# Strassen stages with reused weights, and one block's split weights kept in DRAM

## The chip, the core and the metric

One program runs on one core of a Trainium2 chip. Its engines each run their own instructions in order: TensorE (PE, matrix products), VectorE (DVE), ScalarE (ACT), GpSimd (POOL); SyncE (SP) issues all transfers of this kernel, also in order. DRAM is the memory outside the core, to and from which 16 DMA engines carry data. The metric is the time of one execution on the device in microseconds, lower is better.

## The reference

Three transformer blocks in a row on 1024 tokens of width 1024, all in float32. Cut to its products:

```python
x = x + mix(rms(x) @ w_in) @ w_out                  # block 1: two kinds of attention
x = x + square(relu(rms(x) @ w_up)) @ w_down        # w_up 1024 x 4096
x = rms(x)
q, k, v, ga, gb, pool, su, sv, gates = split(rms(x) @ w_in_2)   # block 2
y = concat(neighborhood(q, k, v), conv(ga * sigmoid(gb)), pooled(pool), gating(su, sv))
x = rms(x + (y * silu(gates)) @ w_out_2)
x = x + rms(mix3(rms(x) @ w_in_3) @ w_out_3)        # block 3
x = x + rms(cross_attention(rms(x), memory))
u = causal_conv3(rms(x) @ w_up_3)                   # 1024 x 5632, gate and value halves
x = x + rms((gelu(gate) * value) @ w_down_3)
```

## The kernel before

Activations lie transposed, 128 features by 1024 tokens a tile, and are worked on in two halves of 512 tokens (h = 0, 1). A float32 product is made of parts: each operand is split into hi (rounded to the matmul's type) and lo (the rest), and `mm3` (L177) issues hi·hi, hi·lo and lo·hi (L179, L180, L181), each of 512 columns. `dense` runs it over 8 feature tiles: 24 matmuls for an output tile of one half.

**Weights.** `chunk` (L147) loads 512 KB of a weight into `raw` (two buffers), ACT copies it to `whi` (L143), DVE or, with `pool_lo`, POOL subtracts to get `wlo` (L145); whi and wlo have two buffers each. Inside `with e.third()` there is a third pair in a pool "wx", opened and closed there. So whi of a chunk can't be written until PE is done with the chunk two before (three before, in third).

**Order.** The program is built under a scheduler that sets each engine's order from a simulated timeline; on the chip every engine then keeps that order and waits on semaphores. A transfer that waits holds all transfers behind it on SP. Transfers report on eight lanes (DMAHW0 to 7 in the listings).

**The stages around the change**, with their place in the trace (us):
- Block 1, up product with Strassen (to 921): first n0 = 6 chunks for each half in the ordinary way (12 units), in which the norm's late steps (`steps`) and, in the second half, the sums of activations that Strassen needs (`right_forms`) and of weights (`left_forms`) are spread one step a unit; then 13 Strassen units of 7 products instead of 8.
- Block 1, down product (921 to 1271): six groups (6, 6, 5, 5, 5, 5 input tiles) of eight output tiles by two halves. `FfnDown.run` loads one chunk of weights for two products, and beside them loads and splits the next group's activations (`nq`, `up`).
- Block 2 (1271 to 1802): gated units, values, q and k for both halves (`glu`, `values`, `qk`), with the convolution of the gated unit as DVE and POOL work beside them; then pooling, gating, the convolution's output, attention with the gates (`silu`), and the output product. It loads 32 different weight chunks, 18 of them twice: 50 loads, 32 of which serve a single product of 24 matmuls. POOL makes the wlo of 24.
- Block 3, up product (2666 to 3123): n0 = 4 pairs of a gate and a value tile in the ordinary way, 16 units of 24 matmuls, then 18 Strassen units of 84; the causal convolution, gelu and the product of gate and value run on ACT and DVE behind each unit (L1897 to L1917), and the result is stored to `upd` in DRAM.
- Block 3, down product (3134 to 3380), inside `e.third()`; the pool "str" of the Strassen stage has just been closed, and "wx" takes memory that it held.

Of the kernel before, what the change touches and what calls it, by code (L numbers as in the profile page):

```python
# [18 lines left out]
P = 128  # L19
# [39 lines left out]
class Env:  # L59
# [87 lines left out]
    def chunk(self, src, shape=(8, P), pool_lo=False):  # L147

        nc = self.nc
        shape = [P] + list(shape)  # L150
        raw = self.wp.tile(shape, F32, tag="raw", name="raw")
        nc.sync.dma_start(raw, src)
        self.turn = (self.turn + 1) % (2 + len(self.wx))
        wp = self.wp if self.turn < 2 else self.wx[0]
        hi, lo = (wp.tile(shape, F32R, tag=t, name=t) for t in ("whi", "wlo"))
        self.split(hi, lo, raw, pool_lo=pool_lo)
        return hi, lo

    def kept(self, src, a, b):
# [191 lines left out]
def block1(e, next_gain):  # L351
# [328 lines left out]
    with ExitStack() as c2:  # L680
# [11 lines left out]
        forms, left = iter(()), iter(())  # L692
        units = [(f, h) for h in range(2) for f in range(n0)]
        wc = e.chunk(io["w1_up"][0])
        for i, (f, h) in enumerate(units):
            if i == n0:
                for _ in steps:
                    pass
                xs = [[a[:, j] for a in acc] for j in range(2)]
                acc.clear()  # L700
                forms, left = right_forms(e, xs, hs, fm), left_forms(e, weight, 0, w, tmp)
            p = e.dense(wc, hs[h])
            if i + 1 < len(units):
                wc = e.chunk(io["w1_up"][units[i + 1][0]])
            act(f, h, p, tmp.tile([P, HALF], F32, tag="c", name="c"))
            next(steps, None)
            next(forms, None)
            if h and f >= n0 - 2:
                next(left, None)
# [31 lines left out]

    return acc, out, down.run(add, end)

# [137 lines left out]


class FfnDown:

# [14 lines left out]

    def run(self, add, end):  # L900

        e, steps, f0 = self.e, iter(()), 0
        for g, n in enumerate(self.groups):
# [4 lines left out]
            for f, h in order:  # L908
                if last or h == 0:
                    w = e.chunk(self.src[f][:, f0 : f0 + n], (n, P))  # L910
                add(f, h, e.dense(w, us[h]), g)
                next(todo, None)
                next(steps, None)
                if last and f == NK - 1:
                    for _ in steps:
                        pass
                    steps = end(h)
# [55 lines left out]

def block2(e, acc, hs, steps, next_gain):
    nc, tc, io = e.nc, e.tc, e.io
# [20 lines left out]
    with ExitStack() as c2:  # L996
# [3 lines left out]
        def glu(h):  # L1000
            for b in range(2):
                pa = e.dense(e.chunk(io["w2_fm"][4 + b]), hs[h])
                pb = e.dense(e.chunk(io["w2_fm"][6 + b], pool_lo=True), hs[h])
                s = e.tsq()
# [4 lines left out]
        def values(h):  # L1009
            ws = [e.chunk(io["w2_tm"][0, q], (4, 256), pool_lo=True) for q in range(2)]  # L1010
            for t in range(4 * h, 4 * h + 4):
# [8 lines left out]
        def qk(g, i, h):  # L1020
            y = qring.next()
            p = e.dense(e.chunk(io["w2_fm"][2 * i + g]), hs[h])
            if i == 0:
# [85 lines left out]
        for b in range(2):  # L1109
            w = e.chunk(io["w2_fm"][8 + b])  # L1110
            x = e.slot("px", (T,))
# [52 lines left out]
        v2 = []  # L1164
        ws = [e.chunk(io["w2_tm"][1, q], (4, 256)) for q in range(2)]
        for t in range(8):
# [41 lines left out]
        for b in range(2):  # L1208
            w = e.chunk(io["w2_fm"][10 + b])
            for h in range(2):  # L1210
# [16 lines left out]
        def silu(f):  # L1227

            w = e.chunk(io["w2_fm"][12 + f])
            for h in range(2):  # L1230
# [26 lines left out]
        def out(f, h):  # L1257
            if h == 0:
                acc.append(e.slot("acc"))
            nc.sync.dma_start(acc[f][:, h], xd[f, :, h])  # L1260
            p = e.dense(e.chunk(io["w2_out"][f], pool_lo=True), [m[h] for m in mix], order)
            nc.vector.tensor_tensor(acc[f][:, h], p, acc[f][:, h], op=ALU.add)
# [244 lines left out]
def block3(e, acc, hs, rest, out):  # L1507
# [412 lines left out]
    with ExitStack() as c2:  # L1920
        tmp = c2.enter_context(tc.tile_pool(name="str", bufs=8))
        new = lambda: tmp.tile([P, HALF], F32, tag="c", name="c")
        n0 = 4
        fm, w = {}, {}
        weight = lambda u, i: io["w3_up"][n0 + u + 22 * i]
        forms, left = iter(()), iter(())
        units = [(b, h) for h in range(2) for f in range(n0) for b in (f, 22 + f)]
        wc = e.chunk(io["w3_up"][0])
        for i, (b, h) in enumerate(units):
            if i == 2 * n0:  # L1930
                for _ in steps:
                    pass
                forms, left = right_forms(e, xn, hs, fm), left_forms(e, weight, 0, w, tmp)
            p = e.dense(wc, hs[h])
            if i + 1 < len(units):
                wc = e.chunk(io["w3_up"][units[i + 1][0]])
            c = new()
# [3 lines left out]
            else:  # L1941
# [3 lines left out]
                put_up(b - 22, h, cg, c)  # L1945
            for _ in range(3):
                next(steps, None)
            next(forms, None)
            if h and i >= len(units) - 2:
                next(left, None)  # L1950
# [40 lines left out]

    with e.third():
        for _ in down.run(add, end):
            pass

# [49 lines left out]
def build(tc, io, out):  # L2045
    with ExitStack() as ctx:
        e = Env(ctx, tc, io)
        acc, hs, rest = block1(e, "norm_g_2")
        acc, hs, rest = block2(e, acc, hs, rest, "mix_pre_norm_3")
        block3(e, acc, hs, rest, out)  # L2050
# [18 lines left out]
```

## Time and profile before

| | us |
|---|---|
| median of three runs | 3396.5 (3394.65 to 3396.74) |
| the profiled execution | 3399.09 |
| its span in the trace | 3397.3 |
| PE busy | 3174.9 (93%) |
| DVE, ACT, POOL busy | 2119.8, 1504.1, 698.0 |

Busy PE is not PE at its best: the granted clock of TensorE has two levels, 2.4 and 1.2 GHz (1.00 and 0.50 of a stretch), and a matmul at the lower takes twice as long and counts as busy all the same. So for a stretch both the count of matmuls (x) and the clock are read. The page's mean granted clock is 0.97.

### The profile page before, as it was taken

Reading aid. Unit: us, or ns where it says so; the run is one execution under the profiler, and the core shown is the slowest. Engines: PE = TensorE matmul, PEld = TensorE weight load, DVE = VectorE, ACT = ScalarE, POOL = GpSimd, SP = SyncE. Lnnn points to the kernel's source line nnn. Section 1 sums busy time; section 2 is a strip of 40 time slices with the busy share of each in tenths; the row PEclk is TensorE's granted clock in tenths of the full one; section 3 lists DMA queues with packets and bytes.
Section 4 is the critical chain, followed back from the end, with each engine's and each line's share of the span. In section 5 each row is a group of like instructions: output and inputs, shape, how many; then the busy total and the mean of one; then the engine's idle time right before and its main releaser. Section 6 shows DMA issues by size and latency. Waiting matters only on the chain.

```text
span 3397.3 us, 43416 instructions
## 1 busy us (share of the span) xinstructions
PE 3174.9 (93%) x16044; PEld 2645.4 (78%) x16044; DVE 2119.8 (62%) x3795; ACT 1504.1 (44%) x2710; POOL 698.0 (21%) x451
## 2 busy tenths in 40 slices
PE   7999999999999998889999899989999989998997
PEld 6789877788888877667677777778887768886886
DVE  7666566654435366965776567666636687886336
ACT  4454453454532123433644565654434444454312
POOL 3000024000000004521444444435333200000001
PEclk9999999999999999899999899999999999998999
DMA  4112134433444234355644122225422432223333
GB/s 130 41 57 61 54 112 155 143 109 109 143 130 131 75 96 136 97 141 178 199 158 127 59 66 66 84 79 180 131 69 99 149 99 83 85 79 100 121 114 102
DMA packets 157572, 369.17 MB, mean 109 GB/s; under 512 B 20912, under 2 KB 29488, under 8 KB 157360
## 3 DMA queue, kind: packets, MB, share of 16 engines
q1 hardware_dynamic: 157360, 366.40, 33.8%
q8 instruction: 126, 2.06, 0.3%
q14 instruction: 86, 0.70, 0.1%
HBM read 286.64 MB, written 72.88 MB: 106 GB/s over the span
## 4 chain that ended last, share of the span: by engine, by line
PE 35%; DVE 9%; ACT 3%; issue 2%; DMA 1%; POOL 1%; SPq 0%; DVEq 0%; ACTq 0%; POOLq 0%
PE ps_d L179 10%; PE ps_d L180 10%; PE ps_d L181 10%; ACT whi L143 1%; DVE act L145 1%; DVE acc L1454 1%; POOL wlo L145 1%; PE ps_s L1737 1%; DVE hE L1723 0%; DVE wlo L145 0%; DVE hSA L1738 0%; DVE acc L1455 0%; DVE pr L1650 0%; DVE ssum L254 0%; PE ps_o L1320 0%
## 5 line engine op out<-in xcount | busy, mean ns | idle before, releaser
L143 ACT ACTIVATE whi<-raw 128x1024 fp32r<-128x1024 f32 (+2 forms) x328 | 317.3, 968 | 711.6 <-PE ps_d L180 601.9
L179 PE MATMUL ps_d<-act,whi 128*128 128x512 f32 x1280 | 512.8, 401 | 24.5 <-DVE acc L316 8.1
L181 PE MATMUL ps_d<-act,wlo 128*128 128x512 f32 x1280 | 508.4, 398 | 20.4 <-DVE wlo L145 19.5
L180 PE MATMUL ps_d<-act,whi 128*128 128x512 f32 x1280 | 508.9, 398 | 6.8 <-DVE act L145 6.7
L145 POOL TENSOR_TENSOR wlo<-raw,whi 128x1024 fp32r<-128x1024 f32 (+1 forms) x134 | 326.0, 2436 | 446.4 <-ACT whi L143 427.9
L179 PE MATMUL ps_d<-up,whi 128*128 128x512 f32 x864 | 337.5, 391 | 11.0 <-ACT whi L143 11.0
L179 PE MATMUL ps_d<-act,ws 128*128 128x512 f32 x868 | 335.0, 390 | 3.8 <-DVE sq L867 1.9
L180 PE MATMUL ps_d<-act,ws 128*128 128x512 f32 x868 | 338.4, 390 | 0.0
L180 PE MATMUL ps_d<-up,whi 128*128 128x512 f32 x864 | 337.2, 390 | 0.0
L181 PE MATMUL ps_d<-up,wlo 128*128 128x512 f32 x864 | 336.8, 390 | 0.0
L181 PE MATMUL ps_d<-act,ws 128*128 128x512 f32 x868 | 336.2, 390 | 0.0
L219 POOL TENSOR_TENSOR rr<-rv,mhalf 128x4 f32<-128x4 f32 (+1 forms) x43 | 45.6, 1060 | 1363.4 <-DVE rv L209 1177.2
L179 PEld LDWEIGHTS ps_d<-act,whi 128*128 128x128 f32 x1280 | 245.8, 192 | 80.8 <-ACT whi L143 14.6
L145 DVE TENSOR_TENSOR wlo<-raw,whi 128x1024 fp32r<-128x1024 f32 (+2 forms) x194 | 212.6, 1096 | 148.8 <-ACT whi L143 148.7
L181 PEld LDWEIGHTS ps_d<-act,wlo 128*128 128x128 f32 x1280 | 245.3, 192 | 73.9 <-DVE wlo L145 22.6
L180 PEld LDWEIGHTS ps_d<-act,whi 128*128 128x128 f32 x1280 | 245.7, 192 | 57.6 <-DVE act L145 7.5
L179 PE MATMUL ps_d<-mix,whi 128*128 128x512 f32 x512 | 201.0, 399 | 6.8 <-DVE acc L635 4.3
L181 PE MATMUL ps_d<-mix,wlo 128*128 128x512 f32 x512 | 201.6, 395 | 5.7 <-POOL wlo L145 5.7
L180 PE MATMUL ps_d<-mix,whi 128*128 128x512 f32 x512 | 203.1, 397 | 1.3 <-DVE mix L145 1.1
L179 PEld LDWEIGHTS ps_d<-up,whi 128*128 128x128 f32 x864 | 163.0, 189 | 45.6 <-ACT whi L143 11.7
L179 PEld LDWEIGHTS ps_d<-act,ws 128*128 128x128 f32 x868 | 163.2, 188 | 38.7 <-ACT ps_d L840 2.7
L181 PEld LDWEIGHTS ps_d<-act,ws 128*128 128x128 f32 x868 | 163.3, 188 | 34.1
(438 smaller groups left out, 6643.3 us busy)
## 6 DMA issues: line engine op xcount, KB each, us to landing
raw<-in_w_up SPq DMA_DIRECT2D x90, 512.0 KB, 3.9
raw<-in_w_fm SPq DMA_DIRECT2D x84, 512.0 KB, 3.8
upd<-c SPq DMA_DIRECT2D x108, 256.0 KB, 2.8
nq<-upd SPq DMA_DIRECT2D x108, 256.0 KB, 2.9
raw<-in_w_out SPq DMA_DIRECT2D x42, 512.0 KB, 3.8
xd<-acc SPq DMA_DIRECT2D x80, 256.0 KB, 2.4
raw<-in_w_down SPq DMA_DIRECT2D x64, 320.0 KB, 3.0
acc<-xd SPq DMA_DIRECT2D x64, 256.0 KB, 5.7
```

The lines of the kernel that those rows point to most:

```text
L143: nc.scalar.activation(hi, src, AF.Copy)
L145: e.tensor_tensor(lo, src, hi.bitcast(F32), op=ALU.subtract)
L179: nc.tensor.matmul(out, lhsT=wh, rhs=xh, start=start, stop=False, skip_group_check=more)
L180: nc.tensor.matmul(out, lhsT=wh, rhs=xl, start=False, stop=False, skip_group_check=more)
L181: nc.tensor.matmul(out, lhsT=wl, rhs=xh, start=False, stop=stop, skip_group_check=more)
L219: self.nc.gpsimd.tensor_tensor(r, v, self.mhalf.broadcast_to([P, n]), op=ALU.pow)
L1454: nc.vector.scalar_tensor_tensor(m, m, g[:, k : k + 1], r, op0=ALU.mult, op1=ALU.mult)
L1737: nc.tensor.matmul(s[:, blk(j, 64)], lhsT=x[:, blk(j)], rhs=xv[:, nb * j : nb * j + nb, 1], start=True, stop=True)
```

## The change

Four parts. (1) Block 1's Strassen stage: the second half's six ordinary units run in the order 4, 5, 0, 1, 2, 3, and a helper `Ahead` keeps the last two chunks, so that units 4 and 5 take the weights that the first half has just used: 10 chunk splits instead of 12. (2) Block 3's: six ordinary pairs instead of four (24 units and 16 Strassen units: 1920 matmuls instead of 1896), the second half starts with the first half's last pair, and two norm steps a unit instead of three. (3) Block 3's down product is no longer in `third`. (4) `SplitStore`: during block 1's down product block 2's 32 chunks are loaded, split by ACT and DVE, and stored as hi and lo, 1 MB each, in DRAM; block 2 then gets a chunk by two loads of 512 KB straight into whi and wlo (`ready`), 50 times, without ACT, DVE or POOL. Of block 2's edits some that repeat the same replacement of `e.chunk(...)` by `store.get(...)` are left out.

```diff
@@ -155,6 +155,17 @@
         return hi, lo
+    def ready(self, src, shape=(8, P)):
+        self.turn = (self.turn + 1) % (2 + len(self.wx))
+        wp = self.wp if self.turn < 2 else self.wx[0]
+        out = []
+        for i, t in enumerate(("whi", "wlo")):
+            w = wp.tile([P] + list(shape), F32R, tag=t, name=t)
+            self.nc.sync.dma_start(w.bitcast(F32), src[:, i].rearrange("p (a b) -> p a b", a=shape[0]))
+            out.append(w)
+        return out
...
@@ -690,8 +701,8 @@
         forms, left = iter(()), iter(())
-        units = [(f, h) for h in range(2) for f in range(n0)]
-        wc = e.chunk(io["w1_up"][0])
+        units = [(f, 0) for f in range(n0)] + [(f - 2 if f > 1 else n0 - 2 + f, 1) for f in range(n0)]
+        ahead = Ahead(e, io["w1_up"], [f for f, h in units])
         for i, (f, h) in enumerate(units):
...
@@ -699,13 +710,12 @@
                 forms, left = right_forms(e, xs, hs, fm), left_forms(e, weight, 0, w, tmp)
-            p = e.dense(wc, hs[h])
-            if i + 1 < len(units):
-                wc = e.chunk(io["w1_up"][units[i + 1][0]])
+            p = e.dense(ahead.get(i), hs[h])
+            ahead.get(i + 1)
             act(f, h, p, tmp.tile([P, HALF], F32, tag="c", name="c"))
             next(steps, None)
             next(forms, None)
-            if h and f >= n0 - 2:
+            if i >= len(units) - 2:
                 next(left, None)
...
@@ -739,7 +749,13 @@
-    return acc, out, down.run(add, end)
+    store = SplitStore(e)
+    with tc.tile_pool(name="pre", bufs=2) as pool:
+        extra = store.steps(pool)
+        rest = down.run(add, end, extra)
+        for _ in extra:
+            pass
+    return acc, out, rest, store
...
@@ -880,6 +896,54 @@
+class Ahead:
+    def __init__(self, e, src, order):
+        self.e, self.src, self.order, self.have = e, src, order, []
+    def get(self, i):
+        if i >= len(self.order):
+            return None
+        f = self.order[i]
+        for g, w in self.have:
+            if g == f:
+                return w
+        w = self.e.chunk(self.src[f])
+        self.have = self.have[-1:] + [(f, w)]
+        return w
+class SplitStore:
+    def __init__(self, e):
+        self.e, io = e, e.io
+        fm = lambda *fs: [("fm", f) for f in fs]
+        tm = lambda i: [("tm", i, q) for q in range(2)]
+        self.keys = fm(4, 6, 5, 7) + tm(0) + fm(0, 2, 1, 3, 8, 9) + tm(1) + fm(*range(10, 20)) + [("out", f) for f in range(NK)]
+        self.src = {"fm": io["w2_fm"], "tm": io["w2_tm"], "out": io["w2_out"]}
+        self.d = e.dram.tile([len(self.keys), P, 2, 1024], F32, name="wsplit")
+    def steps(self, pool):
+        e, nc = self.e, self.e.nc
+        for i, (name, *at) in enumerate(self.keys):
+            src = self.src[name]
+            for j in at:
+                src = src[j]
+            t = pool.tile([P, 2, 1024], F32R, tag="w", name="w")
+            raw = t[:, 1].bitcast(F32)
+            nc.sync.dma_start(raw, src.rearrange("p a b -> p (a b)"))
+            yield
+            e.split(t[:, 0], t[:, 1], raw)
+            nc.sync.dma_start(self.d[i], t.bitcast(F32))
+            yield
+    def get(self, *key, shape=(8, P)):
+        return self.e.ready(self.d[self.keys.index(key)], shape)
 class FfnDown:
...
@@ -897,7 +961,7 @@
-    def run(self, add, end):
+    def run(self, add, end, extra=iter(())):
...
@@ -911,6 +975,8 @@
                 next(steps, None)
+                if g:
+                    next(extra, None)
                 if last and f == NK - 1:
...
@@ -999,15 +1065,15 @@
             for b in range(2):
-                pa = e.dense(e.chunk(io["w2_fm"][4 + b]), hs[h])
-                pb = e.dense(e.chunk(io["w2_fm"][6 + b], pool_lo=True), hs[h])
+                pa = e.dense(store.get("fm", 4 + b), hs[h])
+                pb = e.dense(store.get("fm", 6 + b), hs[h])
                 s = e.tsq()
                 nc.scalar.activation(s, pb, AF.Sigmoid)
                 nc.vector.tensor_tensor(hp[b][:, h], pa, s, op=ALU.mult)
                 next(steps, None)
         def values(h):
-            ws = [e.chunk(io["w2_tm"][0, q], (4, 256), pool_lo=True) for q in range(2)]
+            ws = [store.get("tm", 0, q, shape=(4, 256)) for q in range(2)]
             for t in range(4 * h, 4 * h + 4):
...
@@ -1258,7 +1324,7 @@
             nc.sync.dma_start(acc[f][:, h], xd[f, :, h])
-            p = e.dense(e.chunk(io["w2_out"][f], pool_lo=True), [m[h] for m in mix], order)
+            p = e.dense(store.get("out", f), [m[h] for m in mix], order)
             nc.vector.tensor_tensor(acc[f][:, h], p, acc[f][:, h], op=ALU.add)
...
@@ -1920,20 +1986,19 @@
         new = lambda: tmp.tile([P, HALF], F32, tag="c", name="c")
-        n0 = 4
+        n0 = 6
         fm, w = {}, {}
         weight = lambda u, i: io["w3_up"][n0 + u + 22 * i]
         forms, left = iter(()), iter(())
-        units = [(b, h) for h in range(2) for f in range(n0) for b in (f, 22 + f)]
-        wc = e.chunk(io["w3_up"][0])
+        units = [(b, h) for h in range(2) for f in range(n0) for b in ((f - h) % n0, 22 + (f - h) % n0)]
+        ahead = Ahead(e, io["w3_up"], [b for b, h in units])
         for i, (b, h) in enumerate(units):
             if i == 2 * n0:
                 for _ in steps:
                     pass
                 forms, left = right_forms(e, xn, hs, fm), left_forms(e, weight, 0, w, tmp)
-            p = e.dense(wc, hs[h])
-            if i + 1 < len(units):
-                wc = e.chunk(io["w3_up"][units[i + 1][0]])
+            p = e.dense(ahead.get(i), hs[h])
+            ahead.get(i + 1)
             c = new()
...
@@ -1943,10 +2008,10 @@
                 put_up(b - 22, h, cg, c)
-            for _ in range(3):
+            for _ in range(2):
                 next(steps, None)
             next(forms, None)
-            if h and i >= len(units) - 2:
+            if i >= len(units) - 2:
                 next(left, None)
...
@@ -1989,9 +2054,8 @@
-    with e.third():
-        for _ in down.run(add, end):
-            pass
+    for _ in down.run(add, end):
+        pass
```

The scheduler makes of this on SP, in block 2 around `values` (raw, whi and wlo are weight tiles; wsplit is the new tensor in DRAM; vd2, qkd2 and xd2 are stores of values, q and k, and x), before:

```order
L152 DMA raw_10993<-in_w2_fm 128x1024 [waits DMAHW4_49,DVE_49]
L988 DMA xd2_10512<-acc_8368 128x512 [waits DMAHW5_49,DVE_49]
L988 DMA xd2_10512<-acc_8415 128x512 [waits DMAHW6_49,DVE_49]
L152 DMA raw_11024<-in_w2_fm 128x1024 [waits DMAHW7_49,DVE_49]
L1038 DMA qkd2_10526<-qk_10533 128x512 [waits DMAHW0_49,Activation_49]
L152 DMA raw_11058<-in_w2_fm 128x1024 [waits DMAHW4_49,DMAHW1_49,DVE_49]
L1038 DMA qkd2_10526<-qk_10533 128x512 [waits DMAHW2_49,DVE_49]
L1038 DMA qkd2_10526<-qk_10534 128x512 [waits DMAHW3_49,Activation_49]
L1038 DMA qkd2_10526<-qk_10534 128x512 [waits DVE_49]
L152 DMA raw_11089<-in_w2_fm 128x1024 [waits DMAHW7_49,DMAHW5_49,Pool_49]
```

and now:

```order
L166 DMA whi_11054<-wsplit_7989 128x1024 [waits DMAHW6_49,PE_49]
L166 DMA wlo_11056<-wsplit_7989 128x1024 [waits DMAHW7_49]
L166 DMA whi_11089<-wsplit_7989 128x1024 [waits DMAHW0_49,PE_49]
L1082 DMA vd2_10680<-nt_11050 64x256 [waits DMAHW1_49,Activation_49]
L1082 DMA vd2_10680<-nt_11050 64x256 [waits DMAHW2_49]
L166 DMA wlo_11091<-wsplit_7989 128x1024 [waits DMAHW3_49]
L1054 DMA xd2_10665<-acc_8360 128x512 [waits DMAHW4_49,DVE_49]
L1054 DMA xd2_10665<-acc_8407 128x512 [waits DMAHW5_49,DVE_49]
L166 DMA whi_11130<-wsplit_7989 128x1024 [waits DMAHW6_49,PE_49]
L166 DMA wlo_11132<-wsplit_7989 128x1024 [waits DMAHW7_49,PE_49]
```

A weight is two transfers, and the first waits for PE to leave the chunk two before, where a raw load waited for DVE or POOL to have read the raw tile two before.

On PE, at the end of block 3's last Strassen product (ps_d by ws) and the first products of its down stage (up by whi), before:

```order
L179 MATMUL ps_d_25757<-act_23166,ws_25750 128x512
L180 MATMUL ps_d_25757<-act_23166,ws_25750 128x512
L181 MATMUL ps_d_25757<-act_23166,ws_25750 128x512
L179 MATMUL ps_d_25998<-up_25836,whi_25994 128x512 [waits DMAHW4_49,DMAHW3_49,DMAHW5_49,DMAHW2_49,DMAHW6_49,DMAHW1_49,DMAHW7_49,DMAHW0_49,Activation_49]
L180 MATMUL ps_d_25998<-up_25836,whi_25994 128x512
L179 MATMUL ps_d_26024<-up_25841,whi_25994 128x512
L180 MATMUL ps_d_26024<-up_25841,whi_25994 128x512
L179 MATMUL ps_d_26055<-up_25836,whi_26051 128x512
L180 MATMUL ps_d_26055<-up_25836,whi_26051 128x512
L181 MATMUL ps_d_26055<-up_25836,wlo_26052 128x512
```

and now:

```order
L190 MATMUL ps_d_25797<-act_22858,ws_25792 128x512
L191 MATMUL ps_d_25797<-act_22858,ws_25792 128x512
L192 MATMUL ps_d_25797<-act_22858,ws_25792 128x512
L190 MATMUL ps_d_26034<-up_25875,whi_26030 128x512
L191 MATMUL ps_d_26034<-up_25875,whi_26030 128x512
L192 MATMUL ps_d_26034<-up_25875,wlo_26031 128x512
L190 MATMUL ps_d_26034<-up_25899,whi_26030 128x512
L191 MATMUL ps_d_26034<-up_25899,whi_26030 128x512 [waits DVE_49]
L192 MATMUL ps_d_26034<-up_25899,wlo_26031 128x512
L190 MATMUL ps_d_26034<-up_25928,whi_26030 128x512
L191 MATMUL ps_d_26034<-up_25928,whi_26030 128x512 [waits DVE_49]
L192 MATMUL ps_d_26034<-up_25928,wlo_26031 128x512
```

The wait on all eight lanes and ACT ahead of the first down matmul is gone, and whole products of the down stage follow one another.

On DVE, in the first groups of block 1's down product (wlo: that stage's weights; up: its activations; acc: its sums), before:

```order
L732 TENSOR_TENSOR acc_8415<-ps_d_8835,acc_8415 128x512 [waits PE_49]
L145 TENSOR_TENSOR wlo_8914<-raw_8911,whi_8913 128x640 [waits DMAHW4_49,Activation_49]
L145 TENSOR_TENSOR up_9320<-nq_9318,up_9320 128x512 [waits DMAHW0_49,Activation_49]
L145 TENSOR_TENSOR up_9348<-nq_9346,up_9348 128x512 [waits DMAHW1_49,Activation_49]
L732 TENSOR_TENSOR acc_8026<-ps_d_8861,acc_8026 128x512 [waits PE_49]
L736 TENSOR_TENSOR acc_8026<-acc_8026,sq_8878 128x512 [waits DVE_49]
L145 TENSOR_TENSOR up_9370<-nq_9368,up_9370 128x512 [waits DMAHW3_49,Activation_49]
L145 TENSOR_TENSOR up_9398<-nq_9396,up_9398 128x512 [waits DMAHW4_49,Activation_49]
L732 TENSOR_TENSOR acc_8026<-ps_d_8886,acc_8026 128x512 [waits PE_49]
L145 TENSOR_TENSOR wlo_8970<-raw_8967,whi_8969 128x640 [waits DMAHW5_49,Activation_49]
L736 TENSOR_TENSOR acc_8026<-acc_8026,sq_8903 128x512 [waits DVE_49]
```

and now, with w, a chunk of block 2 that is split in place:

```order
L145 TENSOR_TENSOR wlo_8951<-raw_8948,whi_8950 128x640 [waits DMAHW7_49,Activation_49]
L145 TENSOR_TENSOR up_9370<-nq_9368,up_9370 128x512 [waits DMAHW7_49,Activation_49]
L742 TENSOR_TENSOR acc_8018<-ps_d_8893,acc_8018 128x512 [waits PE_49]
L746 TENSOR_TENSOR acc_8018<-acc_8018,sq_8910 128x512 [waits DVE_49]
L145 TENSOR_TENSOR up_9394<-nq_9392,up_9394 128x512 [waits DMAHW1_49,Activation_49]
L742 TENSOR_TENSOR acc_8018<-ps_d_8920,acc_8018 128x512 [waits PE_49]
L145 TENSOR_TENSOR wlo_9012<-raw_9009,whi_9011 128x640 [waits DMAHW4_49,Activation_49]
L746 TENSOR_TENSOR acc_8018<-acc_8018,sq_8937 128x512 [waits DVE_49]
L145 TENSOR_TENSOR w_9483<-w_9483 128x1024 [waits DMAHW6_49,DMAHW2_49,Activation_49]
L145 TENSOR_TENSOR up_9425<-nq_9423,up_9425 128x512 [waits DMAHW4_49,Activation_49]
L742 TENSOR_TENSOR acc_8075<-ps_d_8954,acc_8075 128x512 [waits PE_49]
L145 TENSOR_TENSOR w_9538<-w_9538 128x1024 [waits DMAHW5_49,DMAHW0_49,Activation_49]
```

Between the old instructions stand the new subtractions, each behind its own load.

## Rows read from the trace of the kernel before

**Rows 1.** The page, engines and groups: busy, mean ns, idle before and its releaser.

```profile
PE 3174.9 (93%) x16044; PEld 2645.4 (78%) x16044; DVE 2119.8 (62%) x3795; ACT 1504.1 (44%) x2710; POOL 698.0 (21%) x451
L143 ACT ACTIVATE whi<-raw 128x1024 fp32r<-128x1024 f32 (+2 forms) x328 | 317.3, 968 | 711.6 <-PE ps_d L180 601.9
L145 DVE TENSOR_TENSOR wlo<-raw,whi 128x1024 fp32r<-128x1024 f32 (+2 forms) x194 | 212.6, 1096 | 148.8 <-ACT whi L143 148.7
```

**Rows 2.** Stretches: us, busy and count of PE, PEld, DVE, ACT, POOL, clock, DMA share, GB/s.

```profile
700.00:800.00 100.00, 100.00 (x443) 82.78 (x442) 44.89 (x67) 50.62 (x94) 0.00 (x0) 1.00 0.34 105
620.00:650.00 30.00, 25.89 (x102) 20.20 (x101) 24.92 (x34) 13.87 (x23) 2.86 (x2) 0.89 0.34 113
2710.00:2790.00 80.00, 65.92 (x277) 52.77 (x276) 70.64 (x122) 39.07 (x63) 1.02 (x1) 0.94 0.30 99
2674.00:2724.00 50.00, 40.52 (x183) 32.62 (x182) 43.67 (x68) 25.72 (x37) 7.61 (x6) 0.96 0.44 146
```

**Rows 3.** PE's waits, 2640 to 2800: engine, line, waited for; us, times, longest.

```profile
PE ps_d L180 <- DVE act L145: 6.7, 1, 6.7
PE ps_d L181 <- DVE wlo L145: 3.9, 1, 3.9
```

**Rows 4.** The stretch around the start of block 3's down product.

```profile
3110.00:3140.00 30.00, 17.02 (x56) 12.91 (x55) 18.19 (x36) 9.67 (x15) 0.00 (x0) 0.72 0.36 118
```

**Rows 5.** The chain of waits there: start, us, what.

```profile
3120.08 0.43 PE ps_d L180
...
3123.48 0.79 ACT c L1897
...
3131.52 2.00 DMA upd<-c
...
3133.59 0.85 ACT whi L143
...
3134.48 0.79 PE ps_d L179
```

**Rows 6.** Stretches: block 1's down, its third group, and three of dense transfers.

```profile
960.00:1210.00 250.00, 250.00 (x1104) 207.02 (x1103) 107.54 (x156) 55.81 (x84) 0.00 (x0) 1.00 0.34 106
1050.00:1104.00 54.00, 54.00 (x240) 44.72 (x239) 33.82 (x51) 12.28 (x19) 0.00 (x0) 1.00 0.53 165
2230.00:2235.00 5.00, 3.92 (x17) 3.77 (x18) 4.33 (x17) 2.52 (x8) 1.85 (x3) 0.50 1.02 415
2330.00:2340.00 10.00, 10.00 (x46) 8.29 (x45) 8.89 (x6) 3.49 (x6) 8.97 (x5) 1.00 1.03 346
10.00:20.00 10.00, 10.00 (x72) 10.00 (x72) 10.00 (x18) 5.42 (x9) 2.97 (x2) 1.00 0.92 282
```

**Rows 7.** Transfers: issues, KB each, median us to landing.

```profile
raw<-in_w_fm SPq DMA_DIRECT2D x84, 512.0 KB, 3.8
nq<-upd SPq DMA_DIRECT2D x108, 256.0 KB, 2.9
xd<-acc SPq DMA_DIRECT2D x80, 256.0 KB, 2.4
acc<-xd SPq DMA_DIRECT2D x64, 256.0 KB, 5.7
```

**Rows 8.** PE's waits, 1268 to 1500 (block 2's first products).

```profile
PE ps_d L181 <- DVE wlo L145: 12.5, 4, 6.1
PE ps_d L179 <- DVE acc L316: 8.1, 1, 8.1
PE ps_s L179 <- ACT pls L143: 7.0, 2, 3.5
PE ps_d L179 <- DVE hp L1006: 6.7, 1, 6.7
PE ps_d L179 <- ACT whi L143: 2.3, 3, 1.0
```

**Rows 9.** DVE in time there: start, us, line, operation.

```profile
1374.25 3.33 DVE L145 TENSOR_TENSOR wlo<-raw,whi 128x1024 fp32r<-128x1024 f32 x1
```

More of the change, by code (lines that the diff above doesn't have):

```diff
@@ L971, in layer_norm, with block2 @@
     nc.vector.tensor_scalar(dst, src, mv[:, 0:1], r, op0=ALU.subtract, op1=ALU.mult)
-def block2(e, acc, hs, steps, next_gain):
+def block2(e, acc, hs, steps, store, next_gain):
     nc, tc, io = e.nc, e.tc, e.io
@@ L1021, in qk @@
             y = qring.next()
-            p = e.dense(e.chunk(io["w2_fm"][2 * i + g]), hs[h])
+            p = e.dense(store.get("fm", 2 * i + g), hs[h])
             if i == 0:
@@ L1109, in block2 @@
         for b in range(2):
-            w = e.chunk(io["w2_fm"][8 + b])
+            w = store.get("fm", 8 + b)
             x = e.slot("px", (T,))
@@ L1164, in block2 @@
         v2 = []
-        ws = [e.chunk(io["w2_tm"][1, q], (4, 256)) for q in range(2)]
+        ws = [store.get("tm", 1, q, shape=(4, 256)) for q in range(2)]
         for t in range(8):
@@ L1208, in block2 @@
         for b in range(2):
-            w = e.chunk(io["w2_fm"][10 + b])
+            w = store.get("fm", 10 + b)
             for h in range(2):
@@ L1227, in silu @@
         def silu(f):
-            w = e.chunk(io["w2_fm"][12 + f])
+            w = store.get("fm", 12 + f)
             for h in range(2):
@@ L2047, in build @@
         e = Env(ctx, tc, io)
-        acc, hs, rest = block1(e, "norm_g_2")
-        acc, hs, rest = block2(e, acc, hs, rest, "mix_pre_norm_3")
+        acc, hs, rest, store = block1(e, "norm_g_2")
+        acc, hs, rest = block2(e, acc, hs, rest, store, "mix_pre_norm_3")
         block3(e, acc, hs, rest, out)
```

## The prediction

> **What bounds the kernel now.** First the page's line of busy time: PE is busy for 3174.9 of 3397.3 us [rows 1], no other engine for more than 62%. So time is won where PE stands still or runs slow, and ACT, DVE or POOL work taken away is worth only what PE waits for it. Next the stretches: in an undisturbed one PE issues 443 matmuls in 100 us at clock 1.00 [rows 2], 0.2257 us each; I call the loss of a stretch its length less 0.2257 us times its count, which takes in waits and the half clock behind them (there a matmul takes 0.43 us [rows 5]). Then PE's waits and the chain at the four places which the change touches.
>
> **Part 1, block 1's Strassen stage.** The stretch at the border of the halves holds 102 matmuls where 132.9 fit: a loss of 30.9 × 0.2257 = 7.0 us [rows 2]. Two units there now take weights that are there, so two copies and two subtractions (0.97 and 1.1 us [rows 1]) leave the engines just when they also make the right forms. The forms themselves stay. I keep 2 us of loss: −5. Bounds: −7, and 0 if the forms alone are what is late.
>
> **Part 2, block 3's.** From 2710 to 2790 PE issues 277 matmuls where 354.4 fit: a loss of 17.5 us [rows 2]. The longest wait there is for the normalised activations, 6.7 us, [rows 3], and DVE is busy 43.67 of 50 us ahead of the border [rows 2]: in eight units (8 × 24 × 0.2257 = 43.3 us of PE) it can't do the norm of the second half and the convolution's work. With twelve units PE takes 65 us, while the norm's part of DVE's work stays as it was; four more units, estimated at 3 us each (a subtraction of 1.1 [rows 1] and as much again twice for the convolution), make it about 56 us. So the norm is in time; reuse takes the new splits away. I keep 2 us: −15.5. Against that stand two Strassen units fewer and eight ordinary ones more, 24 matmuls: +5.4. Sum −10. Bounds −12 (no loss left) and +5 (the loss only moves).
>
> **Part 3, block 3's down product outside `third`.** From 3110 to 3140 PE issues 56 matmuls where 133 fit: a loss of 17.4 us [rows 4]. The chain shows why: PE's last product ends at 3123.5, ACT and DVE make the last output tile, it is stored until 3133.5, and only then ACT copies the first down chunk's whi, on which PE starts at 3134.5 [rows 5]. That whi lies in the pool that was opened on the Strassen stage's memory, and its first write waits for everything that used it; in PE's order the wait on all eight lanes stands at that matmul. Afterwards whi comes from the standing pair, and that wait is gone. Block 1 passes the same border without `third` inside a stretch at full pace. What is late next are activations from `upd`; their last tile is wanted only in a later group. I keep 1 us: −16.4. Two buffers instead of three may cost a little in the down product, but each chunk serves two products there, and group by group block 1 does so at full pace [rows 6]. Bounds −17.4 and 0.
>
> **Part 4a, the store, beside block 1's down product.** 32 chunks are read (512 KB) and written (1 MB): 32 × 1.573 = 50.3 MB. Counted in SP's order, these loads begin behind the stage's 5th weight load and end ahead of its 36th; twelve of these spans hold 36 matmuls and twenty 30, 1032 × 0.2257 = 233 us. The stage itself moves 106 GB/s [rows 6], 24.7 MB in that time. Together 75.0 MB, 322 GB/s. The trace has dense stretches of 282, 346 and 415 GB/s at a DMA share of 0.92 to 1.03 [rows 6]: at 282 the transfers take 266 us, 33 more than PE; at 346 and 415 they fit. The third group is the worst: 8 chunks and 165 GB/s × 54 us make 21.5 MB, 398 GB/s; 62 us at 346, 8 more than PE's 54, and 52 at 415. ACT and DVE have room: a chunk adds some 1 us to each in 7 to 8 us, of which DVE works 3 to 5 [rows 6]. A cycle of a staging buffer (load 3.8 us [rows 7], copy and subtraction 2, store about 5, as two 512 KB pieces in a row) is 11 us, and two buffers turn every 14 to 16. I take +6, nearest to the row of 346. Bounds 0 and +33.
>
> The stretch of 415 GB/s bears on a rule. The Trainium skill, page "DMA: Bandwidth & Descriptors", section "Specifications", gives about 358 GB/s as a core's limit to DRAM; by it the third group would take 60 us, 6 more than PE, and the rest would fit. The trace shows more than that limit for 5 us.
>
> **Part 4b, block 2's reads.** Gone: PE's waits for wlo and whi in the first products, 12.5 + 2.3 us [rows 8], made long where a subtraction stands behind the convolution on DVE or takes 3.33 us [rows 9]; behind each of the four for wlo I count ten matmuls at 0.43 instead of 0.23 us, 8 us. Also less work on DVE and POOL ahead of three other waits: 8.1 for the second half's norm, 7.0 for the pooling, 6.7 for the gated unit [rows 8]; I count 3 of each. Sum −32.
>
> Added: a load now starts when PE leaves the chunk two before, and hi lands 3.8 us later [rows 7], lo behind it: 512 KB at 282 to 346 GB/s are 1.5 to 1.9 us, so about 5.5 us. Before, the raw tile was there early and two splits of 1 us each [rows 1] followed. A single product takes 24 × 0.2257 = 5.4 us, and lo is wanted one matmul pair later: 32 such products, just covered, at 0.2 us each +6. Behind `values` and its like, where both chunks are held to the end, 1.5 us before PE runs dry: three places × 3.6 us, and half clock behind them, 2 each: +17. First loads behind other transfers on SP, at three places, +3: in all 26. Net −6. Bounds: −25 (two thirds of the added hidden by waits that come anyway) and +12 (the other waits stay as they are, and first loads cost twice as much).
>
> **Sum.** −5 − 10 − 16.4 + 6 − 6 = −31.4, on the profiled execution 3399.1 − 31.4 = 3367.7; that execution stands 2.6 us above the median of 3396.5, so 3365.
>
> **Rivals.**
> - *A: the transfers fill up in block 1's down product.* 282 GB/s instead of 346: +33 for +6, so 3392. For it: SP issues in order and a store waits for its split, so the queue isn't always full; mean share was 0.34 and would be around 1 [rows 6]. Against: the large pieces of the store should go like the fast rows.
> - *B: block 2 gains nothing.* Loads begin too late, +12 for −6: 3383. For it: the load's latency now stands in each chain; the waits for norm and pooling have other causes, too.
> - *C, the slower side: whi and wlo land late in SP's queue.* They are issued one behind another and behind waiting stores; acc<-xd, half as large, has a median of 5.7 us where it queues [rows 7]. Each us that wlo lands later than 5.5 costs 32. It decides for slower than before from (31.4 + 6.8) / 32 = 1.2 us on, wlo at 6.7; at 7.6, 3365 + 67 = 3432. Against: 3.8 us is a median over 84 loads in a queue like this.
> - *D: the border of block 3 stays.* The first whi waits for something else as long, for instance its activations: 16 back, 3381. Against: PE's order has full products there, and `up` of the first group is loaded beside the last Strassen unit.
> - *E: transfers run like the fastest row.* 415 GB/s: nothing lost in 4a, 3359. A page of the Trainium skill, "Perfetto Trace Analysis", in its note on use of DRAM above 100%, says that a core alone isn't held to its share and can reach some 120% of it; the row of 415 agrees.
>
> **How the numbers follow.** Forecast 0.48 (its own range 3351 to 3378, from the bounds of the border terms and half of 4b's), E 0.15, B 0.15, A 0.08, C 0.08, D 0.06. About 0.2% (6.8 us, 3389.7) is what a measurement of this kernel can tell. Faster: the forecast, E, D, most of B (0.13) and some of A (0.03), 0.85. Same: the rest of A and B, 0.07. Slower: C, 0.08. The low end is the forecast with 4a at nothing and 4b at −22: 3343. The high end takes in A with 2 us to spare, 3394; C lies outside.
>
> **What would show it.** Of the border terms: 2650 to 2850 without a PE wait of over 2 us; the last Strassen product and the first of down within 2 us. Of 4a: stretches of block 1's down at PE count 443 per 100 us and 300 GB/s or more; fewer matmuls with a DMA share near 1.0 speak for A. Of 4b: DVE and POOL free of wlo in block 2, and PE's waits there named after transfers of whi and wlo, about 3 us behind `values` and under 1 elsewhere; over 1.2 us at each single product is C. I am wrong in kind if the border of block 3 still holds a wait of 10 us, or if block 1's down takes over 10 us longer.

## The result and the profile after

The changed kernel takes 3370.25 us (median of four, 3366.32 to 3377.1) beside 3395.57 for the kernel before in the same measurements: ratio 0.993, interval 0.9918 to 0.9943, 25 us less. 3365 had been forecast, with a range of 3343 to 3394. Its profiled execution has a span of 3370.2 us, 27.1 less than that of before, and the spans can be laid beside each other stage by stage. Stages are cut by PE's matmuls: where the earlier kind ends if two kinds overlap, and block 3's down product where its first matmul stands.

| stage | before | after | difference | forecast |
|---|---|---|---|---|
| start to block 1's up product | 598.6 | 597.8 | −0.8 | 0 |
| its ordinary units (part 1) | 74.2 | 71.7 | −2.5 | −5 |
| its Strassen units | 254.1 | 253.9 | −0.2 | 0 |
| block 1's down product (4a) | 344.0 | 344.9 | +0.9 | +6 |
| block 2 (4b) | 532.0 | 533.0 | +1.0 | −6 |
| block 3 to its up product | 864.8 | 861.8 | −3.0 | 0 |
| up product until the first of down (2, 3) | 466.8 | 441.6 | −25.2 | −26.4 |
| down product | 243.6 | 246.6 | +3.0 | 0 |
| tail | 19.2 | 18.9 | −0.3 | 0 |

Block 3's last two big rows are read together, because with the change the two stages overlap: 12 Strassen matmuls (2.7 us) stand behind the first down product, and before, the half clock behind the wait at the border counted in the down product. Together they are 22.2 us shorter, where 26.4 had been forecast. So block 3 has won nearly all of the time, and the large part of the change, the store of split weights, nothing: it cost next to nothing where it is written and won nothing where it is read. (The 3.0 us in block 3 before its up product stand in no edit; the experiment which only takes `third` away shows 862.2 there too, so the profiled execution of before was slow by that.)

The stretches of the trace after, with columns as in [rows 2]: the first two answer to [rows 2], the third to [rows 4] (the down stage now begins at 3104.7), the others to [rows 6].

```profile
620.00:650.00 30.00, 27.54 (x112) 21.69 (x111) 22.98 (x32) 13.69 (x22) 2.06 (x2) 0.94 0.27 93
2710.00:2790.00 80.00, 76.86 (x332) 62.53 (x331) 68.54 (x116) 37.36 (x55) 0.00 (x0) 0.98 0.30 99
...
3105.00:3205.00 100.00, 100.00 (x443) 82.89 (x442) 44.89 (x71) 39.19 (x64) 0.00 (x0) 1.00 0.44 137
...
920.00:985.00 65.00, 65.00 (x288) 53.84 (x288) 25.97 (x30) 33.00 (x51) 0.00 (x0) 1.00 0.82 293
985.00:1050.00 65.00, 65.00 (x289) 53.78 (x288) 34.77 (x46) 24.16 (x33) 0.00 (x0) 1.00 0.93 332
1050.00:1104.00 54.00, 53.63 (x236) 43.90 (x235) 41.73 (x60) 20.45 (x28) 0.00 (x0) 1.00 1.00 372
...
1160.00:1215.00 55.00, 55.00 (x244) 45.54 (x244) 16.94 (x24) 5.93 (x8) 0.11 (x1) 1.00 0.18 53
```

Read the count first: block 3's border went from 277 to 332 matmuls in 80 us, the first 100 us of its down stage have the 443 of an undisturbed stretch, and block 1's down product keeps its count (288 or 289 in 65 us; 236 for 240 in the third group) while the transfers, 106 GB/s on the mean and 165 in the third group before, rise to 332 and 372 GB/s.

In block 2 PE's waits, 1266 to 1500, have changed their names (us in total, times, longest), and one more stands later, between 1500 and 1850:

```profile
PE ps_d L190 <- DMA whi<-wsplit: 24.8, 6, 9.1
PE ps_d L190 <- DVE acc L327: 5.4, 1, 5.4
PE ps_t L1258 <- DVE xn L1037: 5.1, 1, 5.1
PE ps_s L190 <- ACT pls L143: 4.8, 2, 4.5
PE ps_d L192 <- DMA wlo<-wsplit: 2.8, 4, 1.1
PE ps_d L190 <- DVE hp L1072: 2.3, 1, 2.3
...
PE ps_s L1368 <- DVE mx L1371: 6.6, 1, 6.6
```

Against [rows 8]: the splits' 14.8 us are gone, and 7.0 + 8.1 + 6.7 have become 4.8 + 5.4 + 2.3; in their place stand 24.8 us for whi's transfers. The transfers themselves are not slow. The page after, issues to landing:

```profile
wsplit<-w SPq DMA_DIRECT2D x32, 1024.0 KB, 5.8
...
whi<-wsplit SPq DMA_DIRECT2D x50, 512.0 KB, 4.5
wlo<-wsplit SPq DMA_DIRECT2D x50, 512.0 KB, 5.5
```

What makes PE wait is when they are issued. SP's queue in time, at the waits that end at 1376.5 and 1497.1:

```profile
1366.14 4.14 SPq L1082 DMA_DIRECT2D vd<-nt  x6
1370.38 0.53 SPq L166 DMA_DIRECT2D whi<-wsplit  x1
...
1474.37 16.64 SPq L1114 DMA_DIRECT2D st<-qkd  x32
1491.84 0.34 SPq L166 DMA_DIRECT2D whi<-wsplit  x1
```

In the first case whi is issued 0.8 us before PE runs dry, in the second 3.9 us after it (1488.0), because 32 loads of other data, half a us each, go ahead of it; PE's last product with the chunks before had ended at 1478.7, so here the queue is late and not the buffer.

### The profile page after: what moved, and what is told of

It reads as the page before. It is cut to its first block, busy times and chain, and to the rows that moved or that the text cites. A ratio compares the mean times of both kernels' runs of the same rounds, so it can differ in the third digit from the quotient of the medians.

```text
span 3370.2 us, 43537 instructions
## 1 busy us (share of the span) xinstructions
PE 3177.4 (94%) x16068; PEld 2647.5 (79%) x16068; DVE 2073.7 (62%) x3779; ACT 1480.9 (44%) x2678; POOL 633.5 (19%) x427
## 4 chain that ended last, share of the span: by engine, by line
PE 72%; DVE 12%; DMA 7%; ACT 4%; issue 3%; POOL 1%; SPq 0%; DVEq 0%; ACTq 0%; POOLq 0%
PE ps_d L190 21%; PE ps_d L192 21%; PE ps_d L191 21%; DVE ca L1138 2%; DMA wlo<-wsplit 1%; ACT whi L143 1%; DMA nq<-upd 1%; DVE wlo L145 1%; DVE act L145 1%; POOL wlo L145 1%; PE ps_o L1386 1%; DMA wsplit<-w 1%; DVE acc L1520 1%; PE ps_t L1379 1%; DMA w<-in_w_fm 1%
## 5 line engine op out<-in xcount | busy, mean ns | idle before, releaser
L190 PE MATMUL ps_d<-act,whi 128*128 128x512 f32 x1344 | 540.0, 402 | 40.1 <-DMA whi<-wsplit 24.0
L192 PE MATMUL ps_d<-act,wlo 128*128 128x512 f32 x1344 | 535.2, 400 | 7.6 <-DVE wlo L145 4.0
L191 PE MATMUL ps_d<-act,whi 128*128 128x512 f32 x1344 | 536.2, 399 | 0.1
L143 ACT ACTIVATE whi<-raw 128x1024 fp32r<-128x1024 f32 (+2 forms) x282 | 268.5, 953 | 537.9 <-PE ps_d L191 442.6
L145 POOL TENSOR_TENSOR wlo<-raw,whi 128x1024 fp32r<-128x1024 f32 (+1 forms) x110 | 265.9, 2420 | 384.1 <-ACT whi L143 366.9
L190 PEld LDWEIGHTS ps_d<-act,whi 128*128 128x128 f32 x1344 | 258.7, 192 | 98.7 <-issue 33.4
L191 PE MATMUL ps_d<-act,ws 128*128 128x512 f32 x812 | 316.3, 389 | 0.0
L192 PE MATMUL ps_d<-act,ws 128*128 128x512 f32 x812 | 314.4, 390 | 0.0
L190 PE MATMUL ps_d<-act,ws 128*128 128x512 f32 x812 | 312.7, 390 | 0.4 <-ACT ps_d L856 0.4
L192 PEld LDWEIGHTS ps_d<-act,wlo 128*128 128x128 f32 x1344 | 257.7, 192 | 65.1 <-DMA wlo<-wsplit 6.7
L191 PEld LDWEIGHTS ps_d<-act,whi 128*128 128x128 f32 x1344 | 258.4, 192 | 53.2 <-issue 1.1
L145 DVE TENSOR_TENSOR wlo<-raw,whi 128x1024 fp32r<-128x1024 f32 (+2 forms) x172 | 176.5, 1026 | 108.5 <-ACT whi L143 108.1
L192 PEld LDWEIGHTS ps_d<-up,wlo 128*128 128x128 f32 x864 | 162.3, 188 | 38.0 <-DVE wlo L145 4.2
L190 PEld LDWEIGHTS ps_d<-up,whi 128*128 128x128 f32 x864 | 162.3, 188 | 33.7 <-ACT whi L143 0.6
L191 PEld LDWEIGHTS ps_d<-up,whi 128*128 128x128 f32 x864 | 162.3, 188 | 33.4
```

Of the source, the lines that this page charges most:

```text
L143: nc.scalar.activation(hi, src, AF.Copy)
L145: e.tensor_tensor(lo, src, hi.bitcast(F32), op=ALU.subtract)
L190: nc.tensor.matmul(out, lhsT=wh, rhs=xh, start=start, stop=False, skip_group_check=more)
L191: nc.tensor.matmul(out, lhsT=wh, rhs=xl, start=False, stop=False, skip_group_check=more)
L192: nc.tensor.matmul(out, lhsT=wl, rhs=xh, start=False, stop=stop, skip_group_check=more)
```

## The experiments

Ratios are to the kernel before, with 95% intervals; before is 3395 in all.

**Without the store.** Parts 1 to 3 alone, block 2 as before (in part; against the changed kernel):

```diff
-    store = SplitStore(e)
...
-    return acc, out, rest, store
+    return acc, out, down.run(add, end)
...
-    pa = e.dense(store.get("fm", 4 + b), hs[h])
+    pa = e.dense(e.chunk(io["w2_fm"][4 + b]), hs[h])
```

> Parts 1 to 3 without the store of split weights: block 2 loads and splits its weights as in the kernel before. Theory: the whole gain is in the two Strassen stages (block 3's -22 us, block 1's -2.5), and the store gives nothing: 3368 to 3372 us, within 4 us of the changed kernel's 3370. Rival 1: the store wins block 2's waits for splits, 6 us or more as predicted: 3376 or more. Rival 2: the store costs time that the Strassen stages have earned: 3362 or less.

3369.76 us, ratio 0.9926 (0.9914 to 0.9939), as with the store. Block 2 takes 533.0 us, as in the changed kernel, with the waits for wlo back (12.2 us in five). Both rivals fall: neither 3376 us or more nor 3362 or less was measured.

**The store written and not read** (in part; against the changed kernel):

```diff
-    pa = e.dense(store.get("fm", 4 + b), hs[h])
+    pa = e.dense(e.chunk(io["w2_fm"][4 + b]), hs[h])
```

> As the one without the store, but block 1's down product still loads, splits and stores the 32 chunks; block 2 does not read them and splits its own. What it costs above that one is the price of the writing alone. Theory: transfers at 330 to 370 GB/s fit beside PE: 0 to 2 us. Rival (the prediction's term): 6 us. Rival A: 30 us.

3367.25 us, 0.9918 (0.9904 to 0.9931): no price that can be told from nothing; block 1's down product takes 344.0 us here and without the store. Block 2, which splits its weights again, takes 529.0 us here and 533.0 in the experiment before with the same code, so differences of 4 us between such rows say nothing.

**The store written twice**, on the kernel that does not read it (in part):

```diff
             nc.sync.dma_start(self.d[i], t.bitcast(F32))
+            nc.sync.dma_start(self.d2[i], t.bitcast(F32))
```

> As the one whose store is not read, but each chunk is stored twice, to two tensors in DRAM: 33.6 MB more, 108 MB in 233 us, 466 GB/s if PE is to keep pace. Theory: the transfers were near their end already (share 0.87 to 1.00 at 309 to 372 GB/s), so PE now waits: at 372 GB/s 290 us, 57 more, at 415 27 more; 3394 to 3425 us. Rival: there was much room left: under 3380 us.

3379.07 us, 0.9954 (0.9942 to 0.9967): 11.8 more than written once. The expectation is missed: its theory wanted 27 us or more, and the time lies just inside the rival's range. Block 1's down product takes 362.7 us, 18.7 more. Its stretches show why the sum was too simple:

```profile
1050.00:1104.00 54.00, 54.00 (x240) 44.74 (x239) 31.85 (x46) 14.24 (x21) 0.00 (x0) 1.00 0.95 357
1104.00:1160.00 56.00, 56.00 (x249) 46.39 (x248) 32.68 (x46) 17.48 (x25) 0.00 (x0) 1.00 0.87 323
1160.00:1215.00 55.00, 55.00 (x245) 45.54 (x244) 28.05 (x38) 14.55 (x20) 0.00 (x0) 1.00 0.92 347
1215.00:1290.00 75.00, 61.55 (x246) 46.54 (x245) 63.37 (x92) 32.31 (x46) 10.40 (x8) 0.93 0.85 314
```

The rate stays at 314 to 357 GB/s at a DMA share of 0.85 to 0.95. Whether the transfers bound it or the turn of the two staging buffers isn't shown: from 940 to 1290 SP stands 24.1 us waiting for a staging buffer to be stored. PE keeps its pace while the new transfers fall behind into the last two groups, which the change leaves empty of them (53 GB/s from 1160 to 1215, in the trace after); only where the stage has to end does PE wait. So the write in the change is free with some 100 us of slack behind it (its last store is issued at 1156.0, the stage ends at 1268.3).

**The store alone**, on the kernel before, without parts 1 to 3 (in part):

```diff
+    store = SplitStore(e)
...
-    pa = e.dense(e.chunk(io["w2_fm"][4 + b]), hs[h])
+    pa = e.dense(store.get("fm", 4 + b), hs[h])
```

> The kernel before with part 4 alone: the store written in block 1 and read by two pairs in block 2. Theory: it gives nothing, 3393 to 3398 us. Rival: it is worth the 6 us or more of the prediction by itself and the Strassen parts hide it: 3390 us or less.

3396.23 us, 1.0004 (0.9996 to 1.0013). It gives nothing by itself, as the theory had it. Block 2 takes 533.0 us here too.

**Three pairs in block 2.** The raw buffers, empty there, serve as a third pair (in part; against the changed kernel):

```diff
-        self.turn = (self.turn + 1) % (2 + len(self.wx))
+        self.trio = (self.trio + 1) % 3
...
-            w = wp.tile([P] + list(shape), F32R, tag=t, name=t)
+            w = self.wp.tile([P] + list(shape), F32R, tag=t if self.trio < 2 else "raw", name=t)
```

> The changed kernel, with a third pair of hi and lo in block 2: the two raw buffers, which stand empty there, so a load waits for the chunk three before instead of two. Theory: the waits for whi behind values and at the first gated unit of the spatial gating (24.8 us in six, the longest 9.1) come from loads that can start only when PE runs dry, or stand behind others on SP: 15 to 20 us of them go, 3350 to 3358 us. Rival: the same waits come back under another name (the norm's activations, the pooling, the convolution), because DVE and ACT set that stage: 3365 to 3372 us.

3356.61 us, 0.9894 (0.9879 to 0.9909), 13.6 under the changed kernel and clear of it. Block 2 takes 517.1 instead of 533.0 us. PE's waits, 1266 to 1500:

```profile
PE ps_s L189 <- ACT pls L143: 7.2, 3, 3.1
PE ps_d L189 <- DVE qk L1101: 6.9, 2, 5.7
PE ps_d L189 <- DMA whi<-wsplit: 5.8, 2, 4.6
PE ps_d L189 <- DVE acc L326: 5.4, 1, 5.4
```

19 of the 24.8 us for whi are gone; two other waits, for the pooling and for q and k, have taken part of it back, as the rival had it, but not most. Of the one wait behind the 32 loads half stays, 4.6 us of 9.1; they stand ahead of whi here, too:

```profile
1456.67 17.15 SPq L1113 DMA_DIRECT2D st<-qkd  x32
1474.17 0.34 SPq L165 DMA_DIRECT2D whi<-wsplit  x1
```

Of the other 15.7 us, 1.2 are left: those came of too few buffers.

**Loads issued by GpSimd**, two pairs (against the changed kernel):

```diff
-            self.nc.sync.dma_start(w.bitcast(F32), src[:, i]...)
+            self.nc.gpsimd.dma_start(w.bitcast(F32), src[:, i]...)
```

> The changed kernel, with block 2's loads of hi and lo issued by GpSimd instead of SP, still two pairs. It tells a late start by buffers from a late start by SP's queue. Theory (buffers): behind values the load still starts when PE leaves the chunk, so about 10 of the 24.8 us stay; only the 9.1 us behind 32 other transfers goes; 3360 to 3366 us. Rival (queue): nearly all goes, 3350 to 3356 us. Rival: the loads wait among GpSimd's convolution work or the other way round, 3375 us or more.

3394.98 us, 0.9997 (0.9988 to 1.0006): the third case, 25 more than the changed kernel. Block 2 takes 550.9 us, 17.9 more. PE's waits, 1266 to 1500:

```profile
PE ps_d L190 <- DMA whi<-wsplit: 16.4, 4, 7.1
PE ps_d L190 <- DVE qk L1102: 12.9, 2, 8.4
PE ps_d L190 <- DVE acc L327: 6.6, 1, 6.6
```

One more wait for whi ends just past this window, at 1501.4:

```profile
PE ps_d L190 <- DMA whi<-wsplit: 8.1, 1, 8.1
```

With SP's queue out of the way 24.5 us for whi stay of 24.8, and from 1270 to 1510 the loads wait on GpSimd for PE to leave a buffer:

```profile
POOL whi L166 <- PE ps_d L192: 68.2, 14, 12.1
```

So the buffers are a cause here as well, and the theory's saving of 9.1 us didn't come. But GpSimd's own order is in play in place of SP's, so this run can't say how many of the 24.8 us were the queue's.

**Without `third` alone**, on the kernel before.

```diff
-    with e.third():
-        for _ in down.run(add, end):
-            pass
+    for _ in down.run(add, end):
+        pass
```

> The kernel before with one change: block 3's down product not in third. Theory: the wait of 11.0 us at its first chunk and the half clock around it go (-16), two buffers instead of three cost 3 us in the down product: 3382 to 3384 us. Rival D: something else holds the first product as long: 3393 to 3397. Rival: block 3's whole gain of 22 us is this: 3374 us.

3383.11 us, 0.9966 (0.9954 to 0.9979), as the theory has it. Across the border PE stands still no more:

```profile
3095.00:3125.00 30.00, 30.00 (x134) 24.86 (x133) 22.32 (x42) 14.59 (x25) 0.00 (x0) 1.00 0.45 145
```

Block 3's up and down product together take 698.6 us instead of 710.4.

**Six pairs with reuse alone** (part 2, down still in `third`; in part):

```diff
-        n0 = 4
+        n0 = 6
...
-        units = [(b, h) for h in range(2) for f in range(n0) for b in (f, 22 + f)]
+        units = [(b, h) for h in range(2) for f in range(n0) for b in ((f - h) % n0, 22 + (f - h) % n0)]
...
-            for _ in range(3):
+            for _ in range(2):
                 next(steps, None)
```

> The kernel before with part 2 alone: six ordinary pairs, reuse at the border, two norm steps a unit; block 3's down still in third. Theory: the loss at the border goes as computed, -10 (15.5 saved, 5.4 paid for 24 matmuls), and the wait of 11 us at the down stage stays: 3384 to 3387 us. Rival: the wait behind the Strassen stage grows or shrinks with it: outside 3380 to 3390.

3387.79 us, 0.998 (0.9971 to 0.9989), 7 less, just short of what was expected; the wait of 11.1 us for the first whi stays, and one of 4.5 us ahead of the last Strassen product has come up, 1.9 before.

**Six pairs without reuse, and reuse without six pairs**, in part. The first also takes two norm steps a unit instead of three, the second leaves three:

```diff
-        n0 = 4
+        n0 = 6
...
-            for _ in range(3):
+            for _ in range(2):
                 next(steps, None)
```

```diff
-        units = [(b, h) for h in range(2) for f in range(n0) for b in (f, 22 + f)]
+        units = [(b, h) for h in range(2) for f in range(n0) for b in ((f - h) % n0, 22 + (f - h) % n0)]
```

> As part 2 alone, but without the reuse: six ordinary pairs in the old order, every unit loads and splits its chunk. Theory: the longer first half gives DVE the time for the norm, so nearly all of the gain is here: 3385 to 3389 us. Rival: the two chunks less to split at the border are what counts: 3392 to 3398 us, since 24 matmuls more cost 5.4.

> The kernel before with the reuse alone: four ordinary pairs, the second half starts with the first half's last pair, three norm steps a unit. Theory: DVE is still late with the norm of the second half (6.7 us of wait), only the wait for wlo of 3.8 and a little half clock go: 3389 to 3393 us. Rival: reuse is what counts: 3380 or less.

3397.59 us both, 1.0009 (1.0 to 1.0017) and 1.0006 (0.9997 to 1.0015): neither gives anything. The first expectation is missed, the second too by some us. (The first time lies where its rival put it, but the rival's reason, that reuse is what counts, falls with the second.) PE's waits, 2640 to 2830, first with six pairs, then with reuse:

```profile
PE ps_d L181 <- DVE wlo L145: 6.6, 3, 5.8
PE ps_d L179 <- ACT whi L143: 3.2, 4, 1.2
```

```profile
PE ps_d L180 <- DVE act L145: 5.7, 1, 5.7
PE ps_d L179 <- ACT whi L143: 3.8, 3, 2.4
PE ps_d L179 <- ACT ps_d L840: 3.6, 1, 3.6
```

With six pairs the norm's activations are in time, as computed, and DVE is then late with the wlo of the second half's first units. With reuse those are there, and the activations are late. One wait covers the other, so only both together pay.

**`third` for the last group alone**, on the version with three pairs (in part):

```diff
+            more = ExitStack()
+            if last and late:
+                more.enter_context(e.third())
             for f, h in order:
```

> The kernel with three pairs in block 2, and block 3's down product opening third for its last group alone, when the Strassen stage's memory has long been left. Theory: the wait of 2.3 us for wlo where the last group turns to the second half, and the half clock behind it, go: 3352 to 3355 us, 2 to 4 us under the one with three pairs. Rival: the new pool's memory makes its first write wait again, or the wait comes back at the norm: 3356 us or more.

3357.13 us, 0.9881 (0.9866 to 0.9897). The wait is gone from the trace and the down product takes 243.5 instead of 246.5 us, but the total can't be told from the version with three pairs, and it lies where the rival put it.

## Why the prediction was right, and where not

- **Part 3 was right in its mechanism**: the first whi waited for memory that the Strassen stage had used, and without `third` the 11 us go. From the Strassen units to the end of the down product the loss, as the prediction counts it, falls from 21.3 to 4.8 us, by 16.5 where 16.4 had been forecast. That it fits so well is luck: the border gave more (a wait of 1.9 us just ahead of it went, too), and the cost of two buffers in the down product, set at nothing because block 1 runs so at full pace, is 3 us (246.5 us instead of 243.5 with `third` in the last group). The last group loads a chunk for each single product, which the others don't. The trace after has the wait 6 us before the stage's end; there DVE makes the first half's last norm, and the wlo of the last chunks come between (start, us):

```profile
PE ps_d L192 <- DVE wlo L145: 2.4, 1, 2.4
...
3334.49 2.71 DVE L1520 SCALAR_TENSOR_TENSOR acc<-acc,g_ffn_post_norm,ps_t 128x512 f32<-128x512 f32 x4
3337.12 0.98 DVE L145 TENSOR_TENSOR wlo<-raw,whi 128x640 fp32r<-128x640 f32 x1
3338.02 2.71 DVE L1520 SCALAR_TENSOR_TENSOR acc<-acc,g_ffn_post_norm,ps_t 128x512 f32<-128x512 f32 x4
...
3344.21 0.81 DVE L145 TENSOR_TENSOR wlo<-raw,whi 128x640 fp32r<-128x640 f32 x1
```

- **Part 2**: forecast −10; alone it is 7 (ratio 0.998). The ordinary units took 21.9 us more than their matmuls before (108.6 less 384 × 0.2257) and 10.8 after (140.8 less 130.0): 11.1 saved less 5.4 for the 24 matmuls is −5.7. From 2710 to 2790 I had left 2 us of loss, and 5.1 stay (80 less 332 × 0.2257), among them a wait of 2.0 for wlo and the half clock behind it. This is the largest part of what block 3 fell short of the forecast. The reason given first, DVE's time for the norm, was half of it: reuse is needed as well. Parts 2 and 3 alone make 12.1 + 7.4 of the 25.5 us which parts 1 to 3 make together; part 1 has 2.5 to 4 in the traces, and what is left is within the intervals. (Alone, part 2 also makes the wait ahead of the last Strassen product longer, 4.5 us instead of 1.9; without `third` it goes.)
- **Part 1**: forecast −5; the stage is 71.7 us instead of 74.2, 70.1 to 71.7 in the six experiments that have it, and 74.1 to 74.3 in the five that don't. It was not run alone, so its share of the time is read from this row only.
- **4a, forecast +6, measured +0.9 and, alone, nothing**: rival E in its outcome, not in its rate of 415 GB/s. The third group ran at 372 GB/s, share 1.00, with 236 matmuls recorded instead of 240; one wait of 0.4 us for a wlo stands there. That rate is above the limit of some 358 GB/s which the Trainium skill gives ("DMA: Bandwidth & Descriptors", "Specifications") and under the 120% of it that the Trainium skill's page "Perfetto Trace Analysis", "Roofline", allows a core alone; the measurement agrees with the second. The group had been counted to need 398 GB/s; the transfers that didn't fit went into the groups behind.
- **4b, forecast −6, measured +1**: the failing term. The removed waits were about right: 14.8 us of splits, and 9.3 of the 21.8 us for norm, pooling and gated unit where 9 had been counted. But of the 8 us of half clock only some 5 were there to win: it stands behind two of the four waits for wlo, those of 3.9 and 6.1 us, and not behind the other two. Stretches of before, behind the second and the third, columns as in [rows 2]:

```profile
1396.80:1402.60 5.80, 5.80 (x14) 4.54 (x15) 5.80 (x5) 0.00 (x0) 2.87 (x1) 0.50 0.54 181
1418.40:1422.90 4.50, 4.50 (x20) 3.73 (x21) 4.50 (x4) 1.44 (x2) 2.95 (x1) 1.00 0.72 229
```

Of the added, the loads behind `values` and at one more place came somewhat larger than forecast (3.4, 5.3 and 5.1 us for 3.6 each), but "first loads behind other transfers on SP" were put at 3 us for three places, and the one at 1488 alone is 9.1. Two waits that had been short grew, too: xn to 5.1, mx to 6.6. C didn't happen: single products wait under 1.2 us for lo. The bounds of this term don't follow from their words either: with a third of the added left the sum is −23, with the other waits as they were and first loads twice as dear +6, not −25 and +12.

A term of +6 and one of −6 were both off and cancelled in the sum, which is luck; the forecast's excess of 6 us is mostly parts 1 and 2.

## What to carry to other kernels

Work moved off the engines onto transfers is worth only what its waits were. A load that takes the place of a split can need a buffer more, since it starts only where the last reader leaves: look for memory that the move itself sets free. A pool opened on memory that has just been left inherits the last user's wait; take it later or not at all. Where two late producers end at one border, taking away one can show nothing; try them together before either is given up.

## What the runs showed of the hardware

Reads and writes together ran at 323 to 369 GB/s for 275 us beside PE at full pace (the store written twice, 940 to 1215), without a matmul getting slower: 289 in 65 us as before. On SP 32 transfers took 16.64 us to issue, about half a us each, which counts where a load stands behind them.
